# A residual addition, the last Strassen columns and the last norm's beta, moved between engines in a hybrid decoder layer

## The chip, the cores and the metric

The kernel runs on one core of one Trainium2 chip. The metric is the device time of one execution, in microseconds (us): the median of the timed runs. TensorE (PE) multiplies, VectorE (DVE), ScalarE (ACT) and GpSimd (POOL) work elementwise, SyncE (SP) issues most of the DMAs. Each engine takes its instructions in the order in which the program gives them. POOL also issues DMAs, among them those that add to what their destination holds (`accum_op`).

## The reference, cut to what matters

256 tokens of width 2048 go through one layer in float32: an FFN, a mixer (attention beside a convolution), a second FFN, each followed by a LayerNorm of the residual sum.

```python
x = layer_norm(ALPHA * x + 0.5 * swiglu_ffn(x, w_gate1, w_up1, w_down1), ln1_g, ln1_b)
u = x @ w_in + b_in                       # 2048 x 3328
attn_out, conv_out = ...                  # sliding-window attention, causal depthwise convolution
x = layer_norm(ALPHA * x + concat(attn_out, conv_out) @ w_out + b_out, ln2_g, ln2_b)
x = layer_norm(ALPHA * x + 0.5 * swiglu_ffn(x, w_gate2, w_up2, w_down2), ln3_g, ln3_b)

def swiglu_ffn(x, w_gate, w_up, w_down):  # 2048 -> 5632 -> 2048
    return (silu(x @ w_gate) * (x @ w_up)) @ w_down
```

## The kernel before, in words

**Products.** Each float32 operand is split into a rounded part `hi` and a rest `lo`, and a product is three matmuls: hi by hi, hi by lo, lo by hi (`mm3`, L676 to L678). So each weight tile of 128x1024 ("a unit") is loaded by a DMA into `raw`, cast by ACT into `hi` (L166 or L249) and subtracted by DVE into `lo` (L170 or L252). `Steps` decides the order in which that work is written between the matmuls: at most 7 units ahead (`LEAD`), in rings of 8 `hi`/`lo` buffers and 4 `raw` buffers.

**Strassen sets.** The FFN's matmuls are grouped in `by_sums` into sets. A set of kind C is the plain product of two weight tiles with both token halves: 24 matmuls of 128x512. A set of kind S is a Strassen-Winograd product of the same size with seven products in place of eight: 21 matmuls. Its weights come into a staging tile `more` (four blocks of 128x1024, two sets at a time, `load_set`, L155), and DVE forms the sums of its blocks (L184: `sum`, `more`) and four units from it. `more` lies in the same memory as the token tile `xt` (tag "xt", one buffer). So S sets can run only while the tokens are stored away in DRAM (`sides`, tensor `y`).

**FFN.** The 5632 hidden columns are worked in three parts (`PARTS`: 16, 16 and 12 blocks of 128). Each part runs its up projection in pairs of column groups (`pair`, eight sets each, L1058 takes the sums out of PSUM into `part`), multiplies the gate (L1005, `ht`), turns the result (L1019, `hr`; DMAs to DRAM and back, `far` at L1024 and `hf` at L1026), splits it (`hh` at L1032 on ACT, `hl` at L1033 on DVE), and then multiplies it by the down weights. Parts 0 and 1 do that by `down_by_sums` (eight sets for each two of the four 512-wide output columns, L933, and DMAs that add the result to `y`, L951). The last part does it plainly: the tokens are read back from `y` (`tokens_back`, L467), and `tokens_by` multiplies column by column (PE tile `acc`); each sum goes from PSUM into `xt` (L488) with its statistics (L494). It takes columns 0 and 1 first, of each the first eight blocks (`down_order`). At the end of FFN2 the last eight units of token half 1 (b=1) are held back, so that the norm of half 0 (b=0) lies beside them.

**Start of FFN2.** The first four column groups are plain (PE tile `grp`). Beside them `residuals` turns `xt` into the scaled residual, and stores it: for each of four 512-wide columns it loads a gain row `rg` and a beta row `rb` (L471), ACT scales `rb` (L598) and normalises `xt` (L602), DVE multiplies by `rg` (L592), a DMA from POOL's queue adds `rb` to `xt` in SBUF (L589), and another stores `xt` to `y` (L611). Only when all eight stores are written may the first S set's `more` be loaded; its DMA stands in SP's queue and waits there for the memory of `xt`.

**The end.** `norm_to_rows` does the last LayerNorm. For b=0 DVE does it all: a reciprocal root by three Newton steps (L505 to L515), the centred and scaled rows (L634), scale and beta (L640), and SP stores (L1152). For b=1 ACT takes the root and POOL and ACT share the columns.

Of the kernel before, what the change touches and what calls it, by code (L numbers as in the profile page):

```python
# [9 lines left out]
F32 = mybir.dt.float32  # L10
# [15 lines left out]
KINDS = ("SCCSCSCC", "SCCSCSCC", None)  # L26
BLOCKS = {"S": 7, "C": 4}
# [48 lines left out]
def up_of(g, j0, plain):  # L76
    return 0 if g == plain else 2 if g == j0 // JG else 1

# [264 lines left out]
def hybrid_layer(  # L343
# [29 lines left out]
    def add_ffn(wu, wd, plain):  # L373
        for (j0, j1), kinds in zip(PARTS, KINDS):
            for g in range(j0 // JG, j1 // JG, 2):
                if g < plain:
                    sources.extend(wu[g + i, q, h] for i in range(2) for q in range(4) for h in range(2))
                else:
                    for t, kind in UP[up_of(g, j0, plain)]:
                        add_set(kind, [wu[g + i, t // 2, t % 2] for i in range(2)])  # L380
            if kinds is None:
                sources.extend(wd[c, j0 // 4 + t // 2, t % 2] for c, t in down_order(j1 - j0))
                continue
            for c in range(0, NC_, 2):
                for t, kind in enumerate(kinds, j0 // 2):
                    add_set(kind, [wd[c + i, t // 2, t % 2] for i in range(2)])
# [82 lines left out]
    def row_chunk(r, c, name):  # L469
        t = act.tile([P, 512], F32, tag="bc", name=name, bufs=BC)  # L470
        nc.sync.dma_start(t, rows[r, c * 512 : (c + 1) * 512].partition_broadcast(P))  # L471
        return t
# [93 lines left out]
    def residuals(par, row, more, eng, start, every):  # L566
# [12 lines left out]
        for c in range(NC_):  # L579
            at = start + 1 + c * every  # L580

            def get(c=c, at=at):
                g, be = row_chunk(row, c, f"rg{row}_{c}"), row_chunk(row + 1, c, f"rb{row}_{c}")
                bo = row_chunk(more, c, f"ro{row}_{c}") if more is not None else None
                ys = [xts[0][:, b, c * 512 : (c + 1) * 512] for b in range(2)]

                def on(out, a, b_, op):
                    if eng is nc.vector and op is ALU.add:
                        return lambda: nc.gpsimd.dma_start(out, b_, accum_op=ALU.add)  # L589

                    def work():
                        eng.tensor_tensor(out=out, in0=a, in1=b_, op=op)  # L592
                        if eng is nc.vector:
                            st.vector(0.6)

                    return (lambda: st.soon.append(work)) if st.paced else work

                work = [lambda: nc.scalar.mul(be, be, ALPHA)]  # L598
                if more is not None:
                    work.append(on(be, be, bo, ALU.add))  # L600
                for b in range(2):
                    work.append(lambda b=b: nc.scalar.activation(  # L602
                        ys[b], ys[b], AF.Identity, scale=par[:, b, 3:4], bias=par[:, b, 1:2]
                    ))
# [12 lines left out]
            st.at(at, get, True)  # L617

    def norm_to_rows(b, stats, par, gb, store, kept):
# [24 lines left out]

        if b == 0:
            scaled(0)
            rsqrt(mv[:, 1:2], r, [lambda c=c: scaled(c) for c in range(1, NC_)])
        else:

            s = small.tile([P, 1], F32, tag="rs_v", name="rs_s")  # L650
            w = small.tile([P, 1], F32, tag="rs_w", name="rs_w")
            t = small.tile([P, 1], F32, tag="rs_t", name="rs_t")
            y = small.tile([P, 1], F32, tag="rs_y", name="rs_y")
            nc.scalar.activation(s, mv[:, 1:2], AF.Sqrt, bias=eps)
            nc.vector.tensor_scalar(out=w, in0=mv[:, 1:2], scalar1=EPS, scalar2=-0.5, op0=ALU.add, op1=ALU.mult)
# [9 lines left out]
        if b == 0:  # L665
            for c in range(NC_):
                last(c)
# [12 lines left out]
    def block(x_, k, b):  # L680

        return x_[:, k, b * P : (b + 1) * P] if x_.shape[2] == S else x_[:, 2 * k + b]
# [117 lines left out]
    def tokens_by(lhs, k0, nk, factor, stats, finish, kept=None, lag=0):  # L800
# [7 lines left out]
        order = down_order(nk)  # L808
        skew = 0 if finish is None else SKEW if kept is None else LAST
        held, sums, halves = [], {}, []  # L810
        for n, (c, t) in enumerate(order):
            if t == 0:
                sums[c] = [psB.tile([P, 512], F32, tag="acc", name="acc0")]
                if kept is not None and c in (1, 2):
                    gu = psA.tile([P, 2, 512], F32, tag="gu", name="acc1")
                    sums[c].append(gu[:, 0])
                    halves.append(gu[:, 1, :256])
                else:
                    sums[c].append(psC.tile([P, 512], F32, tag="acc", name="acc1"))
                if kept is not None and c > 0:  # L820
# [6 lines left out]
            behind = lag if n < half - 1 else 0 if n < len(order) - skew else len(order)  # L827
# [89 lines left out]
    def down_by_sums(hh, hl, kinds, factor, side, more):  # L917

        firsts = [sum(BLOCKS[k] for k in kinds[:t]) for t in range(len(kinds))]
        places = {  # L920
            "S": ("11", "22", "12", "S1", "S2", "S3", "S4"),
# [7 lines left out]
        for c in range(0, NC_, 2):  # L929
# [6 lines left out]
            def shared(bank, tmp=tmp):  # L936
# [20 lines left out]
    def ffn(xc, tag, skew, begun, prepare, finish, places, back, kept=None):  # L957
        with tc.tile_pool(name=f"ffn{tag}", bufs=2) as pool:
# [4 lines left out]
            def sums_of(n):  # L963
# [10 lines left out]
                nc.vector.tensor_tensor(out=xs[:, n, 1], in0=part, in1=xs[:, n, 0].bitcast(F32), op=ALU.subtract)  # L974
# [17 lines left out]
            for part, ((j0, j1), kinds) in enumerate(zip(PARTS, KINDS)):  # L992
                n = j1 - j0
                ends = part == len(PARTS) - 1
                count = 2 * n if kinds is None else sum(BLOCKS[k] for k in kinds)
# [20 lines left out]
                def turn(g, ht, hh=hh, hl=hl, kinds=kinds):  # L1016
# [19 lines left out]
                    def split(hf, t):  # L1036
                        full = hf.rearrange("p (t k i) -> p k t i", t=4, k=8)
                        if kinds is None:
                            return parted(8 * g + 4 * t, full[:, 4 * t : 4 * t + 4])
                        kind = kinds[2 * g + t]  # L1040
                        at = sum(BLOCKS[k] for k in kinds[: 2 * g + t])
# [6 lines left out]
                        parted(at, some[:, 1:])  # L1048
                        parted(at + 3, sums)
# [3 lines left out]
                def pair(g, ups, last):  # L1053
# [7 lines left out]
                    def shared(bank):  # L1061
# [7 lines left out]
                        if last is not None:  # L1069
                            last()  # L1070
# [16 lines left out]
                if part == 0:  # L1087
                    if xc is xcat:
                        first_groups(xc, group, lambda: [
                            st.at(2 * m + 1, lambda m=m: sums_of(m), True) for m in range(len(SUMMED))  # L1090
                        ])
                        begun()
                    else:
                        group(0, token_group(xc, skew))
                        begun()
                        group(1, token_group(xc, 0))
                        for m in range(len(SUMMED)):
# [8 lines left out]
                if kinds is not None:  # L1106
                    down_by_sums(hh, hl, kinds, 0.5, sides[xc is not xcat], part > 0 or xc is not xcat)
                    continue
                st.paced = False
                st.at(6, lambda: prepare(pool))  # L1110
                stats = new_stats(f"st{tag}", 1 if kept is None else 2)
                tokens_by((hh, hl), 0, n, 0.5, stats, lambda b: finish(b, stats), kept)
# [13 lines left out]
    def more_places():  # L1126
# [5 lines left out]
        lambda: None if st.x_left else more_places(), lambda: tokens_back(sides[0]))  # L1132
# [10 lines left out]
    def prepare3(pool):  # L1143

        nc.scalar.activation(small.tile([P, 1], F32, tag="rs_v", name="rs_s"), eps, AF.Sqrt)
        for c in range(NC_):
            g = act.tile([P, 512], F32, tag="z", name=f"g3{c}", bufs=ZB)
            nc.sync.dma_start(g, rows[5, c * 512 : (c + 1) * 512].partition_broadcast(P))
            rows3.append((g, row_chunk(6, c, f"b3{c}")))

    def store(b, c, y, queue):
# [5 lines left out]
        lambda: more_places() if len(stored) == 2 * NC_ else None, lambda: tokens_back(sides[1]), kept,  # L1157
# [404 lines left out]
```

## Time and profile before

| | |
|---|---|
| median of 3 runs | 1691.73 us (1691.11 to 1694.22) |
| profiled execution | 1691.87 us, span 1690.1 us |
| PE busy | 1666.7 us, 99% of the span |
| DVE / ACT / POOL busy | 1392.0 (82%) / 925.8 (55%) / 322.1 us (19%) |
| DMA | 378.36 MB, mean 224 GB/s |
| mean granted clock of PE | 0.995 |

The profile is of one execution; its times count from the start of the span. In a timeline row stand start, length, engine, line, operation, and in square brackets how long the engine was idle before it and what ended that. A chain row is a start, a length and what the chain went through. A row of waits reads: engine, tile and line that waited, whom it waited for, total us, times, the longest. FFN1 runs from 4.8 to about 705 us, the mixer to about 960, FFN2 to the end. The last part's down projection begins at 637.8 us in FFN1 and at 1613.5 in FFN2.

### The profile page before, as it was taken

Reading aid. Unit: us, or ns where it says so; the run is one execution under the profiler, and the core shown is the slowest. Engines: PE = TensorE matmul, PEld = TensorE weight load, DVE = VectorE, ACT = ScalarE, POOL = GpSimd, SP = SyncE. Lnnn points to the kernel's source line nnn. Section 1 sums busy time; section 2 is a strip of 40 time slices with the busy share of each in tenths; the row PEclk is TensorE's granted clock in tenths of the full one; section 3 lists DMA queues with packets and bytes.
Section 4 is the critical chain, followed back from the end, with each engine's and each line's share of the span. In section 5 each row is a group of like instructions: output and inputs, shape, how many; then the busy total and the mean of one; then the engine's idle time right before and its main releaser. Section 6 shows DMA issues by size and latency. Waiting matters only on the chain.

```text
span 1690.1 us, 21889 instructions
## 1 busy us (share of the span) xinstructions
PE 1666.7 (99%) x7671; PEld 1383.4 (82%) x7671; DVE 1392.0 (82%) x2049; ACT 925.8 (55%) x1279; POOL 322.1 (19%) x298
## 2 busy tenths in 40 slices
PE   9999999999999999999999999799999999999997
PEld 7888888888888888888888888678888888888886
DVE  7899898888998877758887766699998888988767
ACT  6555555555555554576665564455555555555542
POOL 0100000111100010189997102000000000000100
PEclk9999999999999999999999999899999999999999
DMA  8667677677887667466654668666785666776683
GB/s 303 243 226 238 207 251 237 211 249 238 249 255 237 224 228 258 159 204 184 195 187 151 199 210 256 212 243 217 240 268 195 225 223 210 244 258 205 225 290 102
DMA packets 112239, 378.36 MB, mean 224 GB/s; under 512 B 14080, under 2 KB 14208, under 8 KB 112128
## 3 DMA queue, kind: packets, MB, share of 16 engines
q1 hardware_dynamic: 95760, 332.64, 56.7%
q0 software_dynamic: 16224, 44.05, 10.9%
q8 instruction: 60, 0.98, 0.2%
q14 instruction: 51, 0.42, 0.1%
q10 hardware_dynamic: 144, 0.26, 0.0%
HBM read 348.59 MB, written 26.21 MB: 222 GB/s over the span
## 4 chain that ended last, share of the span: by engine, by line
PE 90%; DVE 4%; DMA 4%; issue 1%; ACT 1%; POOL 0%; SPq 0%; DVEq 0%; ACTq 0%; POOLq 0%
PE sum L676 21%; PE sum L677 21%; PE sum L678 21%; PE acc L676 4%; PE acc L678 4%; PE acc L677 4%; DMA xt<-rb 2%; PE in_c L1213 2%; PE in_a L1213 2%; PE in_q L1213 1%; DVE lo L170 1%; PE grp L677 1%; PE grp L678 1%; PE grp L676 1%; PE in_a L1211 1%
## 5 line engine op out<-in xcount | busy, mean ns | idle before, releaser
L170 DVE TENSOR_TENSOR lo<-raw,hi 128x1024 fp32r<-128x1024 f32 x312 | 367.8, 1221 | 76.5 <-ACT hi L166 75.5
L676 PE MATMUL sum<-hi,xcat 128*128 128x512 f32 x1026 | 399.9, 390 | 9.3 <-DVE ht L1005 8.4
L677 PE MATMUL sum<-lo,xcat 128*128 128x512 f32 x1026 | 399.7, 390 | 1.4 <-DVE lo L170 1.4
L678 PE MATMUL sum<-hi,xcat 128*128 128x512 f32 x1026 | 399.4, 389 | 0.0
L166 ACT CAST hi<-raw 128x1024 fp32r<-128x1024 f32 x312 | 315.5, 1048 | 88.9 <-DMA raw<-in_wu 43.3
L166 ACT CAST hi<-more 128x1024 fp32r<-128x1024 f32 x186 | 168.8, 908 | 178.1 <-DVE more L184 143.4
L249 ACT CAST hi<-raw 128x1024 fp32r<-128x1024 f32 (+1 forms) x180 | 182.6, 1031 | 121.9 <-PE acc L678 57.4
L676 PEld LDWEIGHTS sum<-hi,xcat 128*128 128x128 f32 x1026 | 192.9, 188 | 50.4 <-DVE ht L1005 8.8
L677 PEld LDWEIGHTS sum<-lo,xcat 128*128 128x128 f32 x1026 | 192.9, 188 | 41.5 <-DVE lo L170 1.8
L678 PEld LDWEIGHTS sum<-hi,xcat 128*128 128x128 f32 x1026 | 192.9, 188 | 40.1
L170 DVE TENSOR_TENSOR lo<-more,hi 128x1024 fp32r<-128x1024 f32 x186 | 190.2, 1042 | 32.4 <-ACT hi L166 32.3
L252 POOL TENSOR_TENSOR lo<-raw,hi 128x1024 fp32r<-128x1024 f32 x73 | 175.5, 2424 | 114.7 <-ACT hi L249 107.7
L676 PE MATMUL sum<-hi,hh 128*128 128x512 f32 x488 | 190.1, 390 | 0.5 <-DVE part L933 0.4
L1024 POOL DMA_DIRECT2D far<-hr x88 | 49.4, 577 | 738.6 <-DVE hr L1019 738.5
L678 PE MATMUL sum<-hi,hl 128*128 128x512 f32 x488 | 189.9, 389 | 0.0
L677 PE MATMUL sum<-lo,hh 128*128 128x512 f32 x488 | 189.8, 389 | 0.0
L166 ACT CAST hi<-sum 128x512 fp32r<-128x512 f32 x124 | 77.2, 622 | 171.2 <-DVE sum L184 166.5
L252 DVE TENSOR_TENSOR lo<-raw,hi 128x1024 fp32r<-128x1024 f32 (+1 forms) x107 | 126.1, 1204 | 45.7 <-ACT hi L249 44.9
L1058 DVE TENSOR_TENSOR part<-sum,part 128x512 f32<-128x512 f32 x152 | 100.7, 687 | 23.4 <-PE sum L678 16.4
L676 PEld LDWEIGHTS sum<-hi,hh 128*128 128x128 f32 x488 | 91.6, 188 | 20.6 <-DVE part L933 1.1
L678 PEld LDWEIGHTS sum<-hi,hl 128*128 128x128 f32 x488 | 91.6, 188 | 19.1
L677 PEld LDWEIGHTS sum<-lo,hh 128*128 128x128 f32 x488 | 91.6, 188 | 18.8
(202 smaller groups left out, 2514.2 us busy)
## 6 DMA issues: line engine op xcount, KB each, us to landing
raw<-in_wu SPq DMA_DIRECT2D x272, 512.0 KB, 5.1
raw<-in_wd SPq DMA_DIRECT2D x128, 512.0 KB, 5.0
more<-in_wu SPq DMA_DIRECT2D x76, 512.0 KB, 7.0
raw<-in_win SPq DMA_DIRECT2D x52, 512.0 KB, 4.0
more<-in_wd SPq DMA_DIRECT2D x48, 512.0 KB, 7.4
raw<-in_wout SPq DMA_DIRECT2D x32, 512.0 KB, 3.7
far<-hr POOLq DMA_DIRECT2D x88, 128.0 KB, 2.7
hf<-far POOLq DMA_DIRECT2D x22, 512.0 KB, 3.7
```

The source lines that it names most:

```text
L166: self.nc.scalar.copy(hi, x_)
L170: self.nc.vector.tensor_tensor(out=lo, in0=x_, in1=hi.bitcast(F32), op=ALU.subtract)
L249: nc.scalar.copy(hi, raw)
L252: eng.tensor_tensor(out=lo, in0=raw, in1=hi.bitcast(F32), op=ALU.subtract)
L676: nc.tensor.matmul(ps, s_hi, m_hi, start=start, stop=False)
L677: nc.tensor.matmul(ps, s_hi, m_lo, start=False, stop=False)
L678: nc.tensor.matmul(ps, s_lo, m_hi, start=False, stop=stop)
L1024: nc.gpsimd.dma_start(far[:, :, t].rearrange("f r n -> r f n"), hr[32 * t : 32 * t + 32])
L1058: nc.vector.tensor_tensor(out=out, in0=ps, in1=other, op=ALU.add)
L1211: nc.tensor.matmul(ps[:, :S], w[1][:, n], x1[:, k, 0, :], start=False, stop=k == KT - 1)
L1213: nc.tensor.matmul(ps, w[0][:, n], x1[:, k], start=k == 0, stop=False)
```

## The change: what it does

1. In `residuals` of FFN2 DVE adds `rb` to `xt`, where a DMA from POOL's queue did. POOL keeps the stores to `y`.
2. The last part of each FFN multiplies output columns 0 and 1 by `down_by_sums` with the sets S, C, C, S, C, C; columns 2 and 3 stay plain. The S sets keep a plain block more (kind "L", 8 blocks), since columns 2 and 3 need it. `tokens_back` moves from the last `pair` to the last S set of these columns. The four results stay in SBUF (`part`) and DVE adds them to `xt` (`joins`) with their statistics (`stats_of`). `prepare` moves from step 6 to step 1 of `tokens_by`.
3. The last norm: b=0 takes its root by ACT, DVE and POOL, ACT scales and centres the rows, DVE multiplies by the gain, and the store is a DMA that adds to `out`, which a DMA from POOL's queue has filled with the beta row at the start of FFN2. The gain and beta rows of the last norm are loaded through POOL's and ACT's queues, not SP's. For b=1 the columns 2 and 3 stay in PSUM, no longer 1, 2 and 3, and the two last half columns have PSUM tiles of their own.

The diff, cut to its core:

```diff
-KINDS = ("SCCSCSCC", "SCCSCSCC", None)
-BLOCKS = {"S": 7, "C": 4}
+KINDS = ("SCCSCSCC", "SCCSCSCC", "SCCSCC")
+BLOCKS = {"S": 7, "C": 4, "L": 8}
...
-            if kinds is None:
-                sources.extend(wd[c, j0 // 4 + t // 2, t % 2] for c, t in down_order(j1 - j0))
-                continue
             for c in range(0, NC_, 2):
+                if c > 0 and j1 == JT:
+                    sources.extend(wd[c + i, t // 2, t % 2] for i in range(2) for t in range(j0 // 2, j1 // 2))
+                    continue
...
                 def on(out, a, b_, op):
-                    if eng is nc.vector and op is ALU.add:
-                        return lambda: nc.gpsimd.dma_start(out, b_, accum_op=ALU.add)
-
                     def work():
                         eng.tensor_tensor(out=out, in0=a, in1=b_, op=op)
...
+        minus, root, w, t, y = (small.tile([P, 1], F32, tag=f"rs_{k}", name=f"rs_{k}") for k in "nvwty")
+        nc.scalar.activation(root, mv[:, 1:2], AF.Sqrt, bias=eps)
...
         if b == 0:
-            scaled(0)
-            rsqrt(mv[:, 1:2], r, [lambda c=c: scaled(c) for c in range(1, NC_)])
+            nc.gpsimd.tensor_scalar(out=minus, in0=minus, scalar1=r, scalar2=None, op0=ALU.mult)
+
+            def rest(c):
+                nc.vector.tensor_tensor(out=ys[c], in0=ys[c], in1=gb[c][0], op=ALU.mult)
+                nc.gpsimd.dma_start(out[:P, c * 512 : (c + 1) * 512], ys[c], accum_op=ALU.add)
+
+            for c in range(NC_):
+                nc.scalar.activation(ys[c], ys[c], AF.Identity, scale=r, bias=minus)
+                st.at(c + 2, lambda c=c: rest(c))
...
+        if k0 == 0:
+            order = [x_ for x_ in order if x_[0] > 1]
...
-                if kept is not None and c in (1, 2):
-                    gu = psA.tile([P, 2, 512], F32, tag="gu", name="acc1")
-                    sums[c].append(gu[:, 0])
-                    halves.append(gu[:, 1, :256])
-                else:
-                    sums[c].append(psC.tile([P, 512], F32, tag="acc", name="acc1"))
+                if kept is not None and c == 2:
+                    halves.extend(psA.tile([P, 2, 512], F32, tag="gu", name="acc1")[:, 0, :256] for _ in range(2))
+                sums[c].append(psC.tile([P, 512], F32, tag="acc", name="acc1"))
...
                 add(tmp[3], bank[5], tmp[1])
+                if last is not None:
+                    last()
...
+                if columns < NC_:
+                    y = xts[0][:, 1 - at[0], (c + at[1]) * 512 : (c + at[1] + 1) * 512]
+                    joins[1 - at[0], at[1]] = lambda: nc.vector.tensor_tensor(out=y, in0=y, in1=t, op=ALU.add)
+                    return
...
                         begun()
+                        nc.gpsimd.dma_start(out[:P], rows[6].partition_broadcast(P))
...
-                    pair(g, UP[up_of(g, j0, plain)], back if kinds is None and g + 2 >= j1 // JG else None)
+                    pair(g, UP[up_of(g, j0, plain)])
...
-                st.at(6, lambda: prepare(pool))
+                st.at(1, lambda: prepare(pool))
...
+                def stats_of(b, c):
+                    joins.pop((b, c))()
...
+                for c in range(2):
+                    for b in range(2):
+                        st.at(2 + c + 2 * b, lambda b=b, c=c: stats_of(b, c))
...
-            nc.sync.dma_start(g, rows[5, c * 512 : (c + 1) * 512].partition_broadcast(P))
-            rows3.append((g, row_chunk(6, c, f"b3{c}")))
+            nc.gpsimd.dma_start(g, rows[5, c * 512 : (c + 1) * 512].partition_broadcast(P))
+            rows3.append((g, row_chunk(6, c, f"b3{c}", nc.scalar)))
```

What the engines' own orders show of it, at three places. First POOL's queue at the start of FFN2, before: the additions of `rb` (rb_0 to rb_3, one for each column) stand between the stores to `y` and the turn of the first group pair (`far`, `hf`).

```order
L611 DMA y_138<-xt 128x512 x2
L589 DMA xt<-rb_1_9152 128x512
L1024 DMA far<-hr 32x4x256 x4
L1026 DMA hf<-far 128x1024
L589 DMA xt<-rb_1_9152 128x512
L611 DMA y_138<-xt 128x512 x2
L589 DMA xt<-rb_2_9195 128x512 x2
L611 DMA y_138<-xt 128x512 x2
L589 DMA xt<-rb_3_9244 128x512 x2
L611 DMA y_138<-xt 128x512 x2
L1024 DMA far<-hr 32x4x256 x4
L1026 DMA hf<-far 128x1024
```

The same place of POOL's queue now:

```order
L1176 MEMSET eps 128x1
L1113 DMA out<-in_rows 128x2048
L612 DMA y_138<-xt 128x512 x2
L1044 DMA far<-hr 32x4x256 x4
L1046 DMA hf<-far 128x1024
L612 DMA y_138<-xt 128x512 x6
```

POOL now issues one DMA that fills half of `out` with the beta row, then the stores; the eight additions are gone from its queue.

The second place is DVE at the same time. The additions now stand there, each behind the multiplication of its half and one unit's `lo` (`ht` and `hr` belong to the first group pair's turn):

```order
L256 TENSOR_TENSOR lo_9219<-raw_9142,hi_9218 128x1024
L593 TENSOR_TENSOR xt<-xt,rg_0_9162 128x512
L256 TENSOR_TENSOR lo_9240<-raw_9160,hi_9239 128x1024
L593 TENSOR_TENSOR xt<-xt,rb_0_9164 128x512
L593 TENSOR_TENSOR xt<-xt,rg_0_9162 128x512
L256 TENSOR_TENSOR lo_9265<-raw_9182,hi_9264 128x1024
L593 TENSOR_TENSOR xt<-xt,rb_0_9164 128x512
L593 TENSOR_TENSOR xt<-xt,rg_1_9202 128x512
```

Eight instructions of 128x512 were put into DVE's order between the units that PE will need; nothing else changed its place there.

The third place is DVE at the start of the last part's down projection, in FFN1. Before, behind the transpose `hr` of the last pair came seven plain units, and then the split `hl` of what that transpose gave:

```order
L1005 TENSOR_TENSOR ht<-part 128x8x32 x4
L1019 STREAM_TRANSPOSE hr<-ht 128x1024
L252 TENSOR_TENSOR lo_5543<-raw_5427,hi_5542 128x1024
L252 TENSOR_TENSOR lo_5549<-raw_5445,hi_5548 128x1024
L252 TENSOR_TENSOR lo_5567<-raw_5463,hi_5566 128x1024
L252 TENSOR_TENSOR lo_5585<-raw_5481,hi_5584 128x1024
L252 TENSOR_TENSOR lo_5603<-raw_5546,hi_5602 128x1024
L252 TENSOR_TENSOR lo_5623<-raw_5552,hi_5622 128x1024
L252 TENSOR_TENSOR lo_5641<-raw_5570,hi_5640 128x1024
L1033 TENSOR_TENSOR hl_4472<-hf,hh_4471 128x512 x2
```

Now two units of a C set stand ahead of the gate, and behind the transpose come the nine instructions of the second S set and four units before the same split:

```order
L1077 TENSOR_TENSOR part<-sum,part 128x512 x4
L174 TENSOR_TENSOR lo_5535<-raw_5402,hi_5534 128x1024
L174 TENSOR_TENSOR lo_5538<-raw_5411,hi_5537 128x1024
L1025 TENSOR_TENSOR ht<-part 128x8x32 x4
L1039 STREAM_TRANSPOSE hr<-ht 128x1024
L188 TENSOR_TENSOR sum_5584<-more 128x512
L188 TENSOR_TENSOR sum_5585<-more,sum_5584 128x512
...
L174 TENSOR_TENSOR lo_5611<-more,hi_5610 128x512
...
L174 TENSOR_TENSOR lo_5672<-raw_5550,hi_5671 128x1024
L1053 TENSOR_TENSOR hl_4472<-hf,hh_4471 128x512 x2
```

The transpose moved behind two units, and the split behind some more work of DVE.

More of the change, by code (lines that the diff above doesn't have):

```diff
@@ L77, in up_of, with blocks_of @@
     return 0 if g == plain else 2 if g == j0 // JG else 1
+def blocks_of(columns):
+    return lambda kind: BLOCKS["L" if kind == "S" and columns < NC_ else kind]
 class Steps:
@@ L680, in block @@
     def block(x_, k, b):
-        return x_[:, k, b * P : (b + 1) * P] if x_.shape[2] == S else x_[:, 2 * k + b]
+        if x_.shape[2] == S:
+            return x_[:, k, b * P : (b + 1) * P]
+        kinds = KINDS[-1]
+        return x_[:, sum(4 if y == "C" else 8 for y in kinds[: k // 2]) + 2 * (k % 2) + b]
     def token_mm(ps, lhs, k0, t, nk, b, w):
@@ L826, in tokens_by @@
             held.append((c, t, w))
-            behind = lag if n < half - 1 else 0 if n < len(order) - skew else len(order)
+            behind = len(order) if n >= len(order) - skew else lag if n < half - 1 else 0
             while len(held) > behind:
@@ L915, in by_sums, with down_by_sums @@
                 st.step(0)
-    def down_by_sums(hh, hl, kinds, factor, side, more):
-        firsts = [sum(BLOCKS[k] for k in kinds[:t]) for t in range(len(kinds))]
+    joins = {}
+    def down_by_sums(hh, hl, kinds, factor, side, more, columns, last):
+        firsts = [sum(map(blocks_of(columns), kinds[:t])) for t in range(len(kinds))]
         places = {
-            "S": ("11", "22", "12", "S1", "S2", "S3", "S4"),
+            "S": ("21", "11", "22", "12", "S1", "S2", "S3", "S4")[-blocks_of(columns)("S"):],
             "C": ("21", "11", "22", "12"),
@@ L973, in sums_of, with lower @@
                 nc.scalar.copy(xs[:, n, 0], part)
-                nc.vector.tensor_tensor(out=xs[:, n, 1], in0=part, in1=xs[:, n, 0].bitcast(F32), op=ALU.subtract)
+                def lower():
+                    nc.vector.tensor_tensor(out=xs[:, n, 1], in0=part, in1=xs[:, n, 0].bitcast(F32), op=ALU.subtract)
+                    st.vector(0.6)
+                if st.paced:
+                    st.soon.append(lower)
+                else:
+                    lower()
             def block_sums(out, x_):
@@ L994, in ffn @@
                 ends = part == len(PARTS) - 1
-                count = 2 * n if kinds is None else sum(BLOCKS[k] for k in kinds)
+                columns = 2 if ends else NC_
+                count = sum(map(blocks_of(columns), kinds))
                 hh, hl = (pool.tile([P, count, P], F32R, tag=t, name=f"{t}{part}", bufs=1) for t in ("hh", "hl"))
@@ L1014, in group, with turn @@
                         turn(g // 2, gated.pop())
-                def turn(g, ht, hh=hh, hl=hl, kinds=kinds):
+                def turn(g, ht, hh=hh, hl=hl, kinds=kinds, ends=ends, of=blocks_of(columns)):
                     hr = pool.tile([P, 4, 2 * P], F32, tag="ht", name="hr")
@@ L1103, in ffn @@
                 while g < j1 // JG:
[L1104 removed]
+                    if part == 1 and g == j0 // JG:
+                        for m in range(2, len(SUMMED)):
+                            st.at(4, lambda m=m: st.soon.append(lambda: sums_of(m)))
+                    pair(g, UP[up_of(g, j0, plain)])
                     g += 2
[L1106 to L1107 removed]
+                side = sides[xc is not xcat]
+                down_by_sums(
+                    hh, hl, kinds, 0.5, side, part > 0 or xc is not xcat, columns, (lambda: tokens_back(side)) if ends else None
+                )
+                if not ends:
                     continue
                 st.paced = False
[L1110 removed]
+                st.at(1, lambda: prepare(pool))
                 stats = new_stats(f"st{tag}", 1 if kept is None else 2)
+                def stats_of(b, c):
+                    joins.pop((b, c))()
+                    w = 512 * NC_ // stats[b].shape[1]
+                    for g in range(0, 512, w):
+                        y = xts[0][:, b, c * 512 + g : c * 512 + g + w]
+                        nc.vector.bn_stats(out=stats[b][:, (512 * c + g) // w, :], in_=y)
+                for c in range(2):
+                    for b in range(2):
+                        st.at(2 + c + 2 * b, lambda b=b, c=c: stats_of(b, c))
                 tokens_by((hh, hl), 0, n, 0.5, stats, lambda b: finish(b, stats), kept)
```

53 lines of the change are left out of this document (21 added, 32 removed).

## The prediction

> **What bounds the kernel now.** I read the page's first part and its chain, then PE's waits, then the timelines of PE, SP and DVE around the longest wait.
>
> ```profile
> PE 1666.7 (99%) x7671; PEld 1383.4 (82%) x7671; DVE 1392.0 (82%) x2049; ACT 925.8 (55%) x1279; POOL 322.1 (19%) x298
> ...
> PE sum L676 <- DVE ht L1005: 8.4, 1, 8.4
> PE sum L677 <- DVE lo L170: 1.4, 1, 1.4
> ...
> PE sum L676 <- DVE part L1058: 0.9, 1, 0.9
> PE acc L676 <- DVE st L494: 0.8, 1, 0.8
> ```
>
> PE is busy in 99% of the span: to save time is to save matmuls or PE's few waits. One wait is 8.4 us long and ends in FFN2's first pair.
>
> ```profile
> 1063.47 0.39 PE L678 MATMUL sum<-hi,xcat 128*128 128x512 f32 x1
> 1072.24 0.79 PE L676 MATMUL sum<-hi,xcat 128*128 128x512 f32 x1 [8.38 <-DVE ht L1005]
> 1072.83 0.63 PE L677 MATMUL sum<-lo,xcat 128*128 128x512 f32 x1
> ...
> 1078.64 0.40 PE L676 MATMUL sum<-hi,xcat 128*128 128x512 f32 x1
> ...
> 1088.87 0.39 PE L676 MATMUL sum<-hi,xcat 128*128 128x512 f32 x1
> 1090.68 0.50 PE L677 MATMUL sum<-lo,xcat 128*128 128x512 f32 x1 [1.42 <-DVE lo L170]
> ```
>
> Undisturbed, PE starts a matmul of 128x512 every 0.227 us (48 of them, two C sets, from 49.30 to 60.18 us, in rows shown below). The first S set should start at 1063.70 and starts at 1072.24: 8.54 us late. Behind it PE is slow: 16 matmuls from 1072.24 to 1078.64 take 6.40 us, not 3.63, which is 2.77 more. So the place costs 11.3 us. At 1090.68 PE waits again, for the last unit of the second S set (1.81 less 0.23: 1.58 us). No slow matmuls follow that one.
>
> Why the S set was late, by the chain in order of time and SP's timeline:
>
> ```profile
> 1009.62 9.78 DMA xt<-rb
> 1022.65 9.14 DMA far<-hr
> 1041.79 8.28 DMA xt<-rb
> ...
> 1058.97 2.35 DMA y<-xt
> 1061.78 4.36 DMA more<-in_wu
> ...
> 1044.85 0.33 SPq L110 DMA_DIRECT2D raw<-in_wu  x1
> 1061.40 0.80 SPq L155 DMA_DIRECT2D more<-in_wu  x2
> ```
>
> The additions by DMA run one behind the other on POOL's queue, 8 to 10 us each in these rows, and hold up even the turn (`far`). The last store lands at 1061.3, and only then SP may load `more`, for which its queue was free at 1045.2: 16 us of waiting.
>
> **The change part by part.**
>
> *The residual's additions.* Eight DMAs go; DVE gets eight additions of the size of its multiplications.
>
> ```profile
> 1018.51 0.69 DVE L592 TENSOR_TENSOR xt<-xt,rg 128x512 f32<-128x512 f32 x1 [2.46 <-ACT xt L602]
> ...
> 1036.34 0.49 DVE L982 TENSOR_TENSOR sums<-hf 128x128 f32<-128x128 f32 x2 [2.38 <-DMA hf<-far]
> ...
> 1054.03 1.23 DVE L252 TENSOR_TENSOR lo<-raw,hi 128x1024 fp32r<-128x1024 f32 x1 [0.68 <-ACT hi L249]
> 1066.23 0.69 DVE L184 TENSOR_TENSOR sum<-more 128x512 f32<-128x512 f32 x1 [10.98 <-DMA more<-in_wu]
> ...
> 1089.94 0.68 DVE L170 TENSOR_TENSOR lo<-more,hi 128x512 fp32r<-128x512 f32 x1
> ```
>
> 8 x 0.69 = 5.5 us of DVE. Its idle stretches there, 2.46 and 2.38 us (the second waits for the turn's DMA, which no longer queues behind additions) and some shorter ones, take about 5.1, so DVE is about 0.4 us later. None of the additions waits for anything new: ACT scales `rb` ahead of the multiplication. The last one stands just ahead of the row at 1036.34 and ends near 1037; its store (2.35 us in the chain) lands near 1041, so SP issues `more` at 1045.2, behind its last `raw`, and by the 4.36 us of the chain it lands near 1050, or at 1055 if loads crowd. DVE then meets it as soon as its last plain unit is done, at 1055.26 plus 0.4. Behind each addition on DVE stand units for PE, which ran gapless up to 1063.70 with those idle stretches on DVE; 0.4 us does not starve it.
>
> Is that early enough? The second S set's last unit ended 24.39 us behind the first set's start on DVE (1066.23 to 1090.62). FFN1 runs the same instructions with no such wait ahead of them:
>
> ```profile
> 46.65 0.69 DVE L184 TENSOR_TENSOR sum<-more 128x512 f32<-128x512 f32 x1
> 70.35 0.68 DVE L170 TENSOR_TENSOR lo<-more,hi 128x512 fp32r<-128x512 f32 x1
> ...
> 49.30 0.39 PE L676 MATMUL sum<-hi,xcat 128*128 128x512 f32 x1
> 60.18 0.39 PE L676 MATMUL sum<-hi,xcat 128*128 128x512 f32 x1
> ```
>
> The same 24.4 us, and PE, 13.5 us behind DVE, never waits. In FFN2 DVE led by 6.01 us, by 8.78 with PE's slow stretch, and PE lost 1.58: a lead of 10.4 would have done. Now the lead is 1063.70 - 1055.66 = 8.0, so PE waits 2.4 us, 0.8 more than before. The 0.9 us wait for `part` behind it I leave as it is. Term: -8.54 - 2.77 + 0.8 = **-10.5**. Bounds: with FFN1's lead both small waits go too (-11.3 - 1.6 - 0.9 = -13.8); if `more` comes 3.6 us later, PE waits 6 us and runs slow again (-11.3 + 4.4 + 2.8 = -4.1).
>
> [...]
>
> *The sets.* Of 288 matmuls in each last down projection 6 go (two S sets, 21 for 24). Two FFNs: 12 x 0.227 = **-2.7**, all on PE's path. DVE gets more: for each S set two units and four sums more (2 x 1.0 + 4 x 0.69 = 4.8 us), and for the four results 16 instructions for 8 (5.5), some 15 us in 64, and the block sums of two splits. Parts 0 and 1 run that density:
>
> ```profile
> 448.00:469.00 21.00, 21.00 (x94) 17.40 (x93) 18.50 (x25) 10.95 (x15) 0.87 (x1) 1.00 0.85 269
> 638.00:659.00 21.00, 21.00 (x94) 17.40 (x93) 14.89 (x18) 9.46 (x13) 2.78 (x5) 1.00 0.82 275
> ```
>
> Third column of busy time: DVE has 18.5 of 21 us at S sets (FFN1's part 1) with PE gapless, and 14.9 where the plain columns ran. That fits. The token reload is issued at the second S set; behind it PE has two C sets (10.9 us) and two plain units (5.4) before the first `join`, and DVE has units in hand. It takes:
>
> ```profile
> xt<-y POOLq DMA_DIRECT2D x8, 512.0 KB, 8.9
> ```
>
> *The hand-over to the fifth set.* It needs what the last pair's turn gives. Before, PE came to it after eight plain units; now after S, C, C, S: 90 matmuls, 20.4 us. The turn's chain:
>
> ```profile
> 637.79 0.39 PE L676 MATMUL acc<-hi,hh 128*128 128x512 f32 x1
> 643.52 1.25 DVE L1019 STREAM_TRANSPOSE hr<-ht 128x1024 f32<-128x1024 f32 x1
> 653.04 0.56 POOL L1026 DMA_DIRECT2D hf<-far  x1 [5.65 <-DMA far<-hr]
> 659.31 1.29 DVE L1033 TENSOR_TENSOR hl<-hf,hh 128x512 fp32r<-128x512 f32 x2 [3.18 <-ACT hh L1032]
> ...
> 427.38 0.39 PE L676 MATMUL sum<-hi,hh 128*128 128x512 f32 x1
> 435.49 1.25 DVE L1019 STREAM_TRANSPOSE hr<-ht 128x1024 f32<-128x1024 f32 x1
> 442.46 0.56 POOL L1026 DMA_DIRECT2D hf<-far  x1 [3.09 <-DMA far<-hr]
> 449.29 1.29 DVE L1033 TENSOR_TENSOR hl<-hf,hh 128x512 fp32r<-128x512 f32 x2
> ```
>
> From PE's first down matmul the transpose ended at 7.0 us and the first `hl` at 22.2; at FFN1's part 1, whose order the new one copies (two units ahead of the gate), the transpose ended at 9.4 and `hf` was issued at 15.1, 0.2 earlier than with the slower DMA. PE will want `hl` at 20.9. The first `hl` ended at 22.2 in the one and, held by DVE's order, at 22.6 in the other; the split then needed nothing else. So PE waits 0 (DVE two units faster than at part 1) to 1.7 us; with the late transpose and the slow `far` together 22.2 + 2.4 - 20.9 = 3.7. Bounds 0 and 3.7. In the new order `hl` stands behind some 1.7 us less of DVE's work than at part 1 (four units, for two units and the first half of an S set), so I take the lower part, 0.5 in each FFN: **+1.0**.
>
> *The end.*
>
> ```profile
> 1007.55 0.94 POOL L589 DMA_DIRECT2D xt<-rb  x1 [39.25 <-DVE xt L592]
> ...
> 1674.24 2.74 DVE L640 SCALAR_TENSOR_TENSOR xt<-xt,par,b 128x512 f32<-128x512 f32 x4
> ```
>
> DVE's norm of b=0 (eight long instructions, the last four ending at 1677.0) becomes four, and the two halves get PSUM tiles of their own, so the 0.8 us wait for L494 goes; but then DVE's own steps bind: **-0.4** (0 to -0.8). The rest costs nothing: the fill of `out` comes in the 39 us in which POOL did nothing; SP has eight row loads and four stores less; the gain rows wait on POOL for buffers that the joins free, with nothing behind them until the norm, two column passes later; ACT issues four DMAs of some 0.4 us beside casts. The last adding store, issued near 1678, has some 10 us to the end of the span.
>
> Sum against the profiled execution (1691.87, span 1690.1; the median is 0.14 less): 1691.87 - 10.5 - 2.7 + 1.0 - 0.4 = **1679.3 us**.
>
> **The rivals.**
> 1. The S set is still some us late (DVE behind with its additions, or `more` landing at 1059): PE waits 6 us and the slow stretch comes again. For it: 2.4 us are lacking even in the forecast. Time 1679.3 + 3.6 + 2.8 = 1685.7. Against it: DVE idled for 10.98 us ahead of `more`, so it was not DVE that was late. [...]
> 2. The hand-over takes its upper bound in both FFNs, 3.7 us each: 1679.3 - 1.0 + 7.4 = 1685.7. For it: the last parts' own `far` was the slow one (5.65).
> 3. The change does not free `more`: the stores still land late, behind POOL's turn. Then only the other terms hold: 1691.87 - 2.7 + 1.0 - 0.4 = 1689.8, within 0.2% of before. Against it: in the chain it is the additions, 8 to 10 us each, that fill the queue.
> 4. Slower: the turn's DMAs crowd with four `more` blocks. If the transpose ends at 9.4, `far` takes 2.6 to issue and the chain's longest 9.14 to land, and `hl` comes 6.9 behind `hf` as in the rows, it ends at 28.0; PE waits 7.1 us in each FFN and runs slow for 2.8: 1679.3 - 1.0 + 19.8 = 1698.1. It decides from 6.8 us lost in each FFN (half of 12.6 + 1.0). Against it: the two forerunners shown end `hl` at 22.2 and 22.6, and 9.14 was a `far` behind additions.
>
> **How the numbers follow.** The forecast, with 1674.4 to 1683 about it, gets 0.70; rivals 1 and 2 0.12 and 0.08; rival 3 0.05; rival 4 0.05. The low end is 1691.87 - 13.8 - 2.7 - 0.8 = 1674.6, the high end takes in rivals 1 and 2: 1686. A measurement can tell 0.2% (3.4 us; the three runs lie 3.1 apart). Faster 0.70 + 0.12 + 0.08 = 0.90, same 0.05, slower 0.05.
>
> **What would show it.** After: PE's wait for `ht` at L1005's new line gone, and one of 0 to 4 us for a `lo` near 1077; no DMA `xt<-rb`; SP's first `more` issued near 1045; 12 matmuls fewer; a wait of PE for `hl` or `hh` near 20.4 us into each last down projection. The forecast is wrong if PE stalls over 3.4 us at either place, or waits for a `join` on DVE.

## The result, and the profile after

The changed kernel takes 1676.63 us (median of 4 runs, 1675.45 to 1677.78) against 1692.15 us before: a ratio of 0.9907, with an interval of 0.9890 to 0.9924. The forecast was 1679.3. The profiled execution took 1677.53 us with a span of 1675.7 us and a mean granted clock of 0.998.

The page's first part and the waits of PE, for the changed kernel:

```profile
PE 1660.3 (99%) x7659; PEld 1378.6 (82%) x7659; DVE 1425.0 (85%) x2111; ACT 939.3 (56%) x1302; POOL 323.3 (19%) x302
...
PE acc L678 <- DVE lo L256: 1.3, 2, 0.9
...
PE sum L677 <- DVE part L938: 1.0, 2, 0.8
PE sum L677 <- DVE part L1077: 0.6, 1, 0.6
```

PE has the 12 matmuls less and is 6.4 us less busy, DVE is 33 us busier. The wait of 8.4 us for `ht` is gone, and so are the wait for the second S set's last unit and the wait for the statistics. A new one has come, for `lo` of plain units (L256). It is not the `lo` that the prediction meant (L174, near 1077 us).

The start of FFN2 in the changed kernel, in the timelines of SP, DVE and PE:

```profile
1041.82 0.80 SPq L159 DMA_DIRECT2D more<-in_wu  x2
...
1050.50 0.69 DVE L188 TENSOR_TENSOR sum<-more 128x512 f32<-128x512 f32 x1
1074.22 0.69 DVE L174 TENSOR_TENSOR lo<-more,hi 128x512 fp32r<-128x512 f32 x1
...
1062.76 0.39 PE L677 MATMUL sum<-hi,xcat 128*128 128x512 f32 x1
...
1097.49 0.50 PE L677 MATMUL sum<-hi,xcat 128*128 128x512 f32 x1 [0.57 <-DVE part L1077]
```

SP issues the first `more` at 1041.82 us (1061.40 before). DVE begins the first S set at 1050.50, and PE, without a wait, at 1062.76, where its order puts it. DVE leads by 12.3 us. The first two blocks of `more` had landed at 1050.40 and DVE's last plain unit ended at 1050.37, so neither of the two held it up alone.

Where the time went is read best from where PE's first instruction of each stage starts. All kernels of this study stand in one table, as lengths of stages in us (from the timelines of PE; the columns add up to the span):

| kernel | to FFN1's last down projection | FFN1's last down projection | mixer, plain groups of FFN2 | Strassen pairs of FFN2's first part | to FFN2's last down projection | FFN2's last down projection, to the last matmul's start | tail | span |
|---|---|---|---|---|---|---|---|---|
| before | 637.79 | 67.28 | 347.74 | 99.28 | 461.39 | 66.37 | 10.25 | 1690.1 |
| after | 638.43 | 65.71 | 347.74 | 85.64 | 461.04 | 65.88 | 11.26 | 1675.7 |
| additions alone | 637.44 | 67.09 | 347.72 | 84.32 | 461.04 | 67.36 | 10.23 | 1675.2 |
| additions by DMA again | 638.01 | 65.70 | 347.75 | 98.83 | 461.04 | 64.74 | 11.23 | 1687.3 |
| old last norm | 638.62 | 65.72 | 347.76 | 84.62 | 461.04 | 63.95 | 12.09 | 1673.8 |
| row loads at step 6 | 636.36 | 65.71 | 347.72 | 84.97 | 461.04 | 63.95 | 11.25 | 1671.0 |
| column 1 in PSUM | 638.38 | 65.71 | 347.69 | 84.87 | 461.04 | 65.68 | 10.43 | 1673.8 |
| both of these | 636.96 | 65.71 | 347.74 | 85.12 | 461.06 | 63.96 | 10.35 | 1670.9 |
| beta rows at step 6 | 637.90 | 66.35 | 347.64 | 84.72 | 461.04 | 63.95 | 11.20 | 1672.8 |
| residual 2 steps later | 638.11 | 65.70 | 347.69 | 86.81 | 461.04 | 64.62 | 11.23 | 1675.2 |

The first column differs by 2.3 us between kernels whose instructions there are the same or nearly so. It holds small waits of PE for `part` (L938 in the list above), which come out at 0 to 1.0 us from one profile to the next, and the first 175 us alone differ by 0.9. So one span is no measure for a microsecond. A stage without waits is: 461.04 and 63.95 come again in most kernels. Each row is of one profiled execution, though.

The ratios below are against the kernel before, timed again beside each group of runs: 1691.55 us (additions alone, given back, old last norm, row loads at step 6) and 1691.06 us (the others).

### The profile page after: what moved, and what is told of

Read it like the earlier page. It is cut to its first block, busy times and chain, and to the rows that moved or that the text cites. A ratio compares the mean times of both kernels' runs of the same rounds, so it can differ in the third digit from the quotient of the medians.

```text
span 1675.7 us, 21952 instructions
## 1 busy us (share of the span) xinstructions
PE 1660.3 (99%) x7659; PEld 1378.6 (82%) x7659; DVE 1425.0 (85%) x2111; ACT 939.3 (56%) x1302; POOL 323.3 (19%) x302
## 5 line engine op out<-in xcount | busy, mean ns | idle before, releaser
L174 DVE TENSOR_TENSOR lo<-raw,hi 128x1024 fp32r<-128x1024 f32 x328 | 386.3, 1219 | 73.2 <-ACT hi L170 72.2
L170 ACT CAST hi<-more 128x1024 fp32r<-128x1024 f32 (+1 forms) x198 | 179.8, 908 | 168.0 <-DVE more L188 145.9
L677 PE MATMUL sum<-hi,hh 128*128 128x512 f32 x580 | 226.0, 390 | 1.0 <-DVE part L938 1.0
L174 DVE TENSOR_TENSOR lo<-more,hi 128x1024 fp32r<-128x1024 f32 (+1 forms) x198 | 202.0, 1041 | 28.7 <-ACT hi L170 28.6
L678 PE MATMUL sum<-lo,hh 128*128 128x512 f32 x580 | 225.7, 389 | 0.0
L679 PE MATMUL sum<-hi,hl 128*128 128x512 f32 x580 | 225.7, 389 | 0.0
L253 ACT CAST hi<-raw 128x1024 fp32r<-128x1024 f32 (+1 forms) x156 | 158.5, 1029 | 93.5 <-PE acc L679 44.7
L256 POOL TENSOR_TENSOR lo<-raw,hi 128x1024 fp32r<-128x1024 f32 x73 | 176.0, 2438 | 111.6 <-ACT hi L253 104.7
L677 PEld LDWEIGHTS sum<-hi,hh 128*128 128x128 f32 x580 | 108.9, 188 | 24.8 <-ACT hi L170 1.3
L678 PEld LDWEIGHTS sum<-lo,hh 128*128 128x128 f32 x580 | 108.9, 188 | 22.7 <-DVE lo L174 0.2
L256 DVE TENSOR_TENSOR lo<-raw,hi 128x1024 fp32r<-128x1024 f32 (+1 forms) x83 | 98.2, 1202 | 24.7 <-ACT hi L253 24.1
```

What stands on the lines that cost most here:

```text
L170: self.nc.scalar.copy(hi, x_)
L174: self.nc.vector.tensor_tensor(out=lo, in0=x_, in1=hi.bitcast(F32), op=ALU.subtract)
L253: nc.scalar.copy(hi, raw)
L256: eng.tensor_tensor(out=lo, in0=raw, in1=hi.bitcast(F32), op=ALU.subtract)
L677: nc.tensor.matmul(ps, s_hi, m_hi, start=start, stop=False)
L678: nc.tensor.matmul(ps, s_hi, m_lo, start=False, stop=False)
```

## The experiments

Theory A is that the additions alone free the token tile, and that nearly all of the gain is theirs. Theory D is that two things eat up most of what the sets give in FFN2: the row loads of the last norm, moved from step 6 to step 1, and a conflict between DVE and POOL in the tail.

**The additions alone.** The kernel before, with

```diff
-                    if eng is nc.vector and op is ALU.add:
-                        return lambda: nc.gpsimd.dma_start(out, b_, accum_op=ALU.add)
```

> The kernel before with the residual additions of FFN2 on DVE; the sets and the last norm stay as before. Theory A (the additions alone free the token tile): as in the changed kernel's trace, `more` is issued near 1042 us in place of 1061, PE loses neither the 8.4 us nor the slow stretch nor the wait of the second S set; FFN2's first part gets 13.6 us shorter and the time is 1692.2 - 13.6 = 1678.5 us (1677.5 to 1679.5). Rival B (the lead of 12 us on DVE comes partly from the other edits, and the additions alone give what the prediction's term had): second S set waits 2.4 us, 1692.2 - 10.5 = 1681.7. Rival C (the gain lies in fewer matmuls and the last norm): no less than 1689.

Measured: 1677.47 us (1676.33 to 1679.31), ratio 0.9920 (0.9906 to 0.9933). PE's rows at the first matmul of FFN2's Strassen pairs and at its first down projection:

```profile
1052.25 0.39 PE L673 MATMUL sum<-hi,xcat 128*128 128x512 f32 x1
...
1136.57 0.39 PE L673 MATMUL sum<-hi,hh 128*128 128x512 f32 x1
```

The stage takes 84.32 us, 14.96 less than before, and holds no wait of PE. That is what it takes undisturbed: FFN1's three pairs take 126.48 us (49.30 to 175.78 before), and two thirds of that is 84.32. Theory A holds; rivals B (1681.7) and C (1689 or more) fall. The median is 0.8 us above that of the whole change and the intervals overlap: that the rest of the change is a gain can't be told from these times.

**The additions given back to the DMAs.** The changed kernel with the two lines above put back.

> The changed kernel with the residual additions of FFN2 given back to the DMAs of POOL's queue. Theory A: PE's long wait for `ht`, the slow stretch and the second wait come back, 1676.6 + 13.6 = 1690.2 us (1689 to 1691). Rival B (the prediction's term): 1676.6 + 10.5 = 1687.1. In both, sets and last norm together are worth the difference to the kernel before, by A 1.9 us.

Measured: 1690.91 us (1685.99 to 1693.48), ratio 0.9992 (0.9982 to 1.0003). PE's waits:

```profile
PE sum L680 <- DVE ht L1028: 5.9, 1, 5.9
PE sum L681 <- DVE lo L174: 2.7, 1, 2.7
PE sum L680 <- DVE part L1080: 1.8, 1, 1.8
```

Theory A again: 14.3 us are lost by the medians, within its 1689 to 1691. The single runs spread over 7.5 us, so the stage is the better witness: 98.83 - 85.64 = 13.2, near A's 13.6 and not B's 10.5. Sets and last norm together can't be told from no change without the additions.

**The old last norm.** The changed kernel with `norm_to_rows` as before, the row loads on SP at step 6, plain stores, no fill of `out`:

```diff
-                        nc.gpsimd.dma_start(out[:P], rows[6].partition_broadcast(P))
...
-                st.at(1, lambda: prepare(pool))
+                st.at(6, lambda: prepare(pool))
```

> The changed kernel with the whole last norm as before: Newton steps and all eight row instructions of b=0 on DVE, plain stores by SP, no fill of `out`, the eight row loads by SP at step 6 of the last columns. Only columns 2 and 3 of b=1 stay in PSUM, as in the changed kernel. Theory D (the row loads at step 1 delay the last weight loads, and column 1 in SBUF costs the tail 1.0 us by a conflict of DVE with POOL): PE's two waits for `lo` (1.65 us) go, the tail behind the last matmul keeps its 11.3 us, DVE's eight instructions may bring the 0.8 us wait for the statistics back: 1676.6 - 1.65 + 0 to 0.8 = 1675.0 to 1675.8 us. Rival E (the adding stores are what lengthened the tail): tail 10.3 again as well, 1674.0. Rival F (the new last norm is a gain): 1677.5 or more.

Measured: 1675.59 us (1673.91 to 1675.66), ratio 0.9905 (0.9889 to 0.9920). The last projection fell to 63.95 us, as D had it, with no wait of PE in it. The tail, which D had left at 11.3, grew to 12.09, since DVE came 0.8 us late to the last sums with the eight long instructions of b=0. D's total holds (1675.0 to 1675.8), but with the 0.8 us in the tail and not in a wait of PE. Two of the rows of its tail, from POOL and DVE:

```profile
1664.72 0.75 POOL L660 TENSOR_SCALAR rs_t<-rs_y,rs_w 128x1 f32<-128x1 f32 x1 [49.78 <-DVE rs_y L659]
...
1665.88 1.73 DVE L641 SCALAR_TENSOR_TENSOR xt<-xt,par,b 128x512 f32<-128x512 f32 x1
```

They are as long as in the changed kernel (below), with plain stores. So rival E falls, and F too: apart from its row loads, the new norm is worth 0.84 us of the tail (12.09, less the 11.25 of the next kernel), and in the changed kernel the row loads cost more.

**The row loads at step 6.** The changed kernel with the `st.at(6, ...)` of the diff above and nothing else.

> The changed kernel with the row loads of the last norm (and the root's table load on ACT) at step 6 of the last columns, not step 1. Theory D (256 KB broadcasts for each row, issued from ACT near 1632 us, delay the last raw weights): PE's two waits for `lo` near 1650 us (0.63 and 1.02) go, 1676.6 - 1.65 = 1675.0 us. Rival G (DVE is late there because of the four joins and their statistics): both waits stay, 1676.6. Rival H (the rows then come too late for the norm of b=0): ACT or DVE waits for `g` or `b` behind 1657 us and the time is 1677 or more.

Measured: 1673.55 us (1672.73 to 1675.13), ratio 0.9897 (0.9883 to 0.9910). FFN2's last projection takes 63.95 us, 1.93 less, without a wait of PE. D holds for this part. G falls, the joins being where they were, and H (1677 or more) falls too.

**Only the beta rows at step 6.**

```diff
-            rows3.append((g, row_chunk(6, c, f"b3{c}", nc.scalar)))
+            st.at(5, lambda g=g, c=c: rows3.append((g, row_chunk(6, c, f"b3{c}", nc.scalar))))
```

> The changed kernel with only the four beta rows loaded at step 6; the gain rows (POOL's queue) and the root's table load on ACT stay at step 1. Theory D1 (the bytes of the four beta rows crowd out the weight loads): FFN2's last down projection takes 63.95 us, not 65.88, no wait for `lo` is left, 1676.6 - 1.9 = 1674.7 us. Rival D2 (ACT's table load of 1.28 us ahead of the casts makes the units late): a wait of 0.5 us or more stays, 65 us or more. Rival D3 (the one gain row loaded early does it): unchanged 65.9.

Measured: 1674.55 us (1673.63 to 1677.19), ratio 0.9903 (0.9888 to 0.9919), and 63.95 us again: D1. ACT and PE of the changed kernel at that place, then the DMA issues in 14 us there, of the changed kernel and of this one (KB each, median us from issue to landing):

```profile
1631.96 1.35 ACTq L475 DMA_DIRECT2D b<-in_rows  x3
...
1639.95 1.05 ACT L253 CAST hi<-raw 128x1024 fp32r<-128x1024 f32 x1 [4.35 <-DMA raw<-in_wd]
...
1649.74 0.50 PE L678 MATMUL acc<-lo,hh 128*128 128x512 f32 x1 [0.47 <-DVE lo L256]
1652.25 0.50 PE L678 MATMUL acc<-lo,hh 128*128 128x512 f32 x1 [0.85 <-DVE lo L256]
```

```profile
raw<-in_wd SPq DMA_DIRECT2D x5, 512.0 KB, 7.7
b<-in_rows ACTq DMA_DIRECT2D x4, 256.0 KB, 9.7
```

```profile
raw<-in_wd SPq DMA_DIRECT2D x6, 512.0 KB, 4.4
```

The four beta rows, written to all partitions, are 1 MB. Beside them a weight tile takes 7.7 us to land, not 4.4. ACT stands 4.35 us for one; DVE, with the joins in its order, doesn't catch up, and ten microseconds later PE waits twice. The table load on ACT (D2) and the early gain row (D3) were left in place, and no wait is left: both fall.

What it costs is not fixed. Four kernels of the table have all row loads at step 1, and their last projection in FFN2 takes 65.88, 65.68, 64.74 and 64.62 us: 0.7 to 1.9 us over the 63.95. What sets the size wasn't tried.

**Column 1 of b=1 in PSUM.** The join of that column writes to the free half of a PSUM tile, from where its statistics and the last norm take it:

```diff
+                    kept[1, 1] = [ends_[0][:, 1]]
...
-                    joins[1 - at[0], at[1]] = lambda: nc.vector.tensor_tensor(out=y, in0=y, in1=t, op=ALU.add)
+                    joins[1 - at[0], at[1]] = lambda to=y: nc.vector.tensor_tensor(out=to, in0=y, in1=t, op=ALU.add)
```

> The changed kernel, but the join of b=1's column 1 writes its sum into a free half of a PSUM tile, so that DVE's last-norm instructions on that column have one operand in SBUF, not two. Theory D (DVE with two SBUF operands and POOL hold each other up): the L641 instruction of 1.73 us on that column falls to about 0.70, POOL's first step of the root from 0.76 to 0.34, the tail behind the last matmul from 11.26 to 10.25 us, the time by 1.0 to 1675.6 us; the two waits for `lo` stay. Rival E (the adding stores lengthen the tail): 11.26 us and 1676.6 stay.

Measured: 1675.49 us (1674.42 to 1676.56), ratio 0.9906 (0.9892 to 0.9921). The tail's rows on POOL and DVE, first in the changed kernel, then here:

```profile
1666.70 0.76 POOL L653 TENSOR_SCALAR rs_t<-rs_y,rs_w 128x1 f32<-128x1 f32 x1 [1.69 <-DVE rs_y L652]
1667.78 1.26 POOL L667 TENSOR_TENSOR xt<-xt,g 128x512 f32<-128x512 f32 x1
...
1666.50 0.73 DVE L635 SCALAR_TENSOR_TENSOR xt<-xt,par,g 128x512 f32<-128x512 f32 x1
1667.86 1.73 DVE L641 SCALAR_TENSOR_TENSOR xt<-xt,par,b 128x512 f32<-128x512 f32 x1
1669.51 0.74 DVE L641 SCALAR_TENSOR_TENSOR xt<-acc,par,b 128x512 f32<-128x512 f32 x1
```

```profile
1665.62 0.34 POOL L653 TENSOR_SCALAR rs_t<-rs_y,rs_w 128x1 f32<-128x1 f32 x1 [1.22 <-DVE rs_y L652]
1666.29 1.26 POOL L667 TENSOR_TENSOR xt<-xt,g 128x512 f32<-128x512 f32 x1
...
1666.74 1.41 DVE L641 SCALAR_TENSOR_TENSOR xt<-acc,par,b 128x512 f32<-128x512 f32 x2
```

In the changed kernel the DVE instruction with two operands in SBUF (`xt` and `b`) starts 0.08 us behind POOL's multiplication, runs for 1.73 us and ends 0.55 us behind it; the same instruction with `acc` takes 0.74. POOL's step `rs_t` in its turn starts behind DVE's first one of that kind and takes 0.76 us. Neither is slow by itself: in the kernel before, with POOL idle, four DVE instructions with both operands in SBUF took 2.74 us (the L640 row in the prediction), and `rs_t`, beside a DVE instruction on `acc`, 0.34. With column 1 in PSUM both are short again and the tail is 10.43 us, 0.83 less. Theory D holds, with 0.83 for its 1.0; E falls. This is a reading of the stage: the median is 1.1 us lower, which lies within the spread of the runs.

**Both.** Row loads at step 6 and column 1 in PSUM.

> The changed kernel with the row loads at step 6 and with column 1 of b=1 in PSUM. Theory D: the two places are apart, so both gains hold: the last part's down projection takes 63.95 us as with the late row loads alone, the tail 10.25 us, and the time is 1673.6 - 1.0 = 1672.6 us, under both kernels. Rival E: no more than the late row loads alone, 1673.6.

Measured: 1672.73 us (1672.39 to 1677.03), ratio 0.9897 (0.9879 to 0.9914); the stages show both gains, 63.96 and 10.35 us. By its median it is the shortest of all kernels here, but the interval overlaps that of the changed kernel and of the late row loads. That it is faster than those rests on the stages.

**The residual two steps later.**

```diff
-        x2, "2", BEHIND, lambda: residuals(par2, 3, None, nc.vector, 1, 2), prepare3,
+        x2, "2", BEHIND, lambda: residuals(par2, 3, None, nc.vector, 3, 2), prepare3,
```

> The changed kernel with `residuals` begun two steps of PE (5.4 us) later in FFN2. Tests the prediction's figure that DVE must lead PE by 10.4 us at the first S set. In the changed kernel DVE begins that set 0.3 us behind `more`'s landing near 1049.0 and leads by 12.3. Theory A: `more` lands near 1054.5, DVE leads by 6.8 to 8, so PE waits 2.4 to 3.6 us for the last unit of the second S set, and for nothing at the first set; time 1676.6 + 2.4 to 3.6 = 1679 to 1680.2, and 2.8 more if PE then runs slow. Rival I (the lead is not what binds): no wait, 1676.6. Rival J (later additions delay the units of the plain groups too): PE waits before the first S set.

Measured: 1677.60 us (1676.87 to 1680.50), ratio 0.9924 (0.9902 to 0.9946). DVE at the first S set and at the second one's last unit, and PE there:

```profile
1052.27 0.69 DVE L188 TENSOR_TENSOR sum<-more 128x512 f32<-128x512 f32 x1 [2.24 <-DMA more<-in_wu]
1076.01 0.68 DVE L174 TENSOR_TENSOR lo<-more,hi 128x512 fp32r<-128x512 f32 x1
...
1075.98 0.39 PE L677 MATMUL sum<-hi,xcat 128*128 128x512 f32 x1
1076.75 0.50 PE L678 MATMUL sum<-lo,xcat 128*128 128x512 f32 x1 [0.38 <-DVE lo L174]
```

`more` was issued 3.0 us later and landed 1.8 later, not 5.4. So the expected wait of 2.4 to 3.6 us didn't come, and the time lies under the 1679 to 1680.2 that was expected: DVE leads by 10.1 us (PE's first S set is at 1051.50 + 10.88 = 1062.38). The rule itself can still be tried with this lead. The prediction's 10.4 gives a loss of 0.3 us, and 10.6, which a right count of the slow matmuls gives (next section), a loss of 0.5. PE came 0.77 us behind its last matmul, so it lost 0.54. Theory A's rule holds, with another lead than it took. Rival I would have no wait at all, and for J PE shows no wait ahead of the first S set.

## Why the prediction was right

**The additions (predicted -10.5 us, bounds -13.8 to -4.1; measured -13.64 in the changed kernel, -14.96 alone).** The mechanism was right: the additions by DMA held the stores, the stores held `more`. The stall of 8.54 us and the slow stretch went. (The prediction's "8 to 10 us each" holds for five of the eight additions, which took 7.7 to 10.3 us to land; the other three took 3.3 to 4.4.) The step that was mis-sized is DVE's start of the first S set. The prediction put it at 1055.66, which is its old end of the plain units plus 0.4; it came at 1050.50, and PE's first S set began at 1062.76, for the 1063.70 of the prediction. That `more` would land near 1050 was right (1050.40); that DVE would be at its plain units until 1055.66 was not. So the lead is 12.3 us, not 8.0, and the second S set waits 0, not 2.4. By the rows, DVE's plain units had been late in part for the same reason as `more`. The first turn's `hf` on POOL's queue, before and after:

```profile
1032.48 0.56 POOL L1026 DMA_DIRECT2D hf<-far  x1 [8.95 <-DMA far<-hr]
```

```profile
1023.19 0.57 POOL L1046 DMA_DIRECT2D hf<-far  x1 [5.32 <-DMA far<-hr]
```

It comes 9.3 us earlier. DVE waited 2.38 us for it and began its block sums at 1036.34; now it begins them at 1032.69, without a wait, so that the eight units behind are earlier too: the last ends at 1050.37, before at 1055.26. That is 3.7 of the 4.9 us. (This is read from the two traces; no run tries it by itself, and where the other 1.2 come from stays open.) The prediction gave the additions the idle time of DVE that it could name, 2.46 and 2.38 us, but left the rest of DVE's old times as they were. The bound of -13.8 was too narrow, since more than the named waits was lost: 99.28 - 84.32 = 14.96. By the starts of PE's matmuls these are 11.55 at the first S set, 1.74 at the second and 1.67 about the wait for `part`. The slow stretch was miscounted: from 1072.24 to 1078.64 there are 15 matmuls, not 16, so it cost 6.40 - 3.40 = 3.00 us, not 2.77, and the lead that DVE needs comes out at 10.6, not 10.4. In the changed kernel the wait for `part` stays; with the uneven matmuls about it, it costs the 1.32 by which its stage is longer than with the additions alone.

No run shows by itself that a wait of 2.4 us costs only itself, as the sum has it, and none shows a limit at the 3.4 us of stalling with which the forecast was to be wrong. In their place the runs showed this. At the second S set's last unit, behind waits of 0.38 us (residual two steps later), 1.42 us (before) and 2.72 us (additions given back), the next matmul starts 0.34 us on and those behind it 0.22 to 0.24 us apart. At the first S set, behind 5.87 us (additions given back), most start 0.43 us apart, not 0.227, from 1068.38 to 1071.89: 3.51 - 8 x 0.227 = 1.7 us lost, not the 2.8 that the bound of -4.1 and rival 1 take for 6 us. A shorter wait of that kernel, of 1.8 us, has slow matmuls behind it too (last section).

**The sets (predicted -2.7, -1.36 in each FFN).** In FFN1's last projection they gave 67.28 - 65.71 = 1.57 us, and in FFN2, with late row loads, as much (66.37 - 63.95 = 2.42, of which about 0.8 is the wait for the statistics). In the changed kernel FFN2 keeps 0.49. By count it is 1.36; where the 0.2 more come from stays open.

**The hand-over to the fifth set (predicted +1.0; measured 0).** The changed kernel's rows on PE, DVE and POOL:

```profile
1598.56 0.39 PE L677 MATMUL sum<-hi,hh 128*128 128x512 f32 x1
...
1605.21 1.25 DVE L1039 STREAM_TRANSPOSE hr<-ht 128x1024 f32<-128x1024 f32 x1
...
1611.97 0.58 POOL L1046 DMA_DIRECT2D hf<-far  x1 [2.91 <-ACT hi L170]
...
1617.62 1.28 DVE L1053 TENSOR_TENSOR hl<-hf,hh 128x512 fp32r<-128x512 f32 x2
...
1618.96 0.39 PE L677 MATMUL sum<-hi,hh 128*128 128x512 f32 x1
```

The transpose ends 7.9 us into the projection, not at 9.4, `hf` is issued at 13.4, and the first `hl` ends at 19.7, against 20.9 needed. In FFN1 the rows are the same to 0.1 us. PE waits for neither. The estimate took the slower of its two forerunners for the transpose.

**The end (predicted -0.4; measured +1.0 in the tail, +1.9 in the last columns by the row loads (0.7 to 1.9 over the kernels that have them early), and -0.8 for the wait that went).** This was the step that failed. "The rest costs nothing" was wrong for the four DMAs that ACT issues: it counted ACT's time for them and not their bytes, beside weight loads that FFN2's last columns live on (7.7 us to land beside those bytes, 4.4 without). And the prediction followed only b=0 and the halves. That b=1's column 1 left PSUM it did not cost, and that cost 0.83 us.

The rows of the tail show it: where POOL began first DVE took 1.73 us for 0.74, and where DVE began first POOL took 0.76 for 0.34. With column 1 in PSUM both are short; what lies behind that, no run shows.

So the sum came out near by errors of both signs: the additions gave 3.1 us more than forecast (13.64 for 10.5) and FFN1's last projection 0.7 more (1.57 for 1.36 - 0.5), while FFN2's last projection and its tail, forecast at -1.36 + 0.5 - 0.4 = -1.26, came out at -0.49 + 1.01 = +0.52. (The other stages add +0.3: 0.64 more ahead of FFN1's last projection, 0.35 less behind FFN2's first part.) That 1676.63 lies so near 1679.3 is in part luck.

## What to carry to other kernels

When a DMA queue is what holds an engine, look at everything that stands behind it: freeing POOL's queue here brought the first `more` forward by 19.6 us, but also the turn's `hf` by 9.3 us. Move the whole order forward, not only the wait that the profile names. A load "issued for free" still takes bytes (here 1 MB, beside which a weight tile took 7.7 us to land, not 4.4); look at what lands beside it and when its reader needs it. When data move from PSUM to SBUF, count the operands in SBUF of each DVE instruction that runs beside POOL: here 1.73 us with two, 0.74 with one.

## What the runs showed of the hardware

The length of a wait alone did not decide whether PE ran slow behind it. In the kernel with the additions given back to the DMAs, PE waited 2.7 us at 1086.8 and 1.8 us at 1109.1. The windows, with PE's busy time first and the granted clock third from the end:

```profile
1085.00:1088.00 3.00, 1.18 (x5) 1.00 (x6) 2.79 (x5) 3.00 (x4) 0.00 (x0) 1.00 0.00 0
...
1109.00:1113.00 4.00, 3.91 (x10) 3.13 (x11) 2.58 (x5) 3.39 (x6) 0.00 (x0) 0.57 0.58 220
```

Behind the longer wait the clock was full, behind the shorter one it was 0.57 in the next 4 us, with seven matmuls 0.43 us apart. Nor was the slow stretch of one length: 6.4 us behind the wait of 8.4 us before (1072.24 to 1078.64), about 3.5 us behind the wait of 5.9 us here (1068.38 to 1071.89). What decides either stays open; no run here varies it.
